# Moving raw-weight loads and cached-key loads in the wide-projection stage, and cutting the first weight part and the last output tile in halves

## Chip, cores and metric

The kernel runs on one core of a Trainium2 chip. The metric is the time of one execution in device microseconds; the median of several executions is compared. Besides that, one execution of the kernel is recorded by the hardware profiler, and all views of engines, waits and transfers come from that one.

The core has a matrix engine (TensorE, PE in the profile, with its weight loads as PEld), VectorE (DVE), ScalarE (ACT), GpSimd (POOL) and SyncE (SP). Each engine works through its own instructions in order. SyncE computes nothing here: it issues DMAs. A DMA can be issued from ScalarE's stream as well.

## The reference, cut to what matters

One step of a streaming encoder layer: 1024 frames of a new stream (the prompt) and 64 frames of a running stream (the sample), width 1024. All tokens go through one wide input projection of 6144 columns, two attention branches, and an output projection with a residual.

```python
h = rms_norm(x, norm_w) @ w_in                    # 1024 -> 6144 columns
sb_q, sb_k, sb_v, sb_z, cb_q, cb_k, cb_v, cb_z, g_sb, g_cb = jnp.split(h, SPLIT_POINTS, axis=-1)
...
o_sb = stick_breaking(q, k, v, q_pos, k_pos)      # branch A, 8 heads of 64
o_cb = band_attention(q, k, v, ..., rel_bias)     # branch B, 8 heads of 64
b_sb = (o_sb * jax.nn.silu(z_sb)) @ w_proj_sb
b_cb = (o_cb * jax.nn.silu(z_cb)) @ w_proj_cb
h = jax.nn.sigmoid(g_sb) * b_sb + jax.nn.sigmoid(g_cb) * b_cb
y = x + h @ w_out
```

For the sample, keys and values of 512 past frames (`cache_sb_k`, `cache_sb_v`, `cache_cb_k`, `cache_cb_v`) stand ahead of the new ones. Besides `y`, the keys and values of the new frames are outputs.

## The kernel before

The program is one straight list of instructions for each engine; loops are unrolled when it is built. Everything is computed to near float32 accuracy with a faster matmul type (`F32R`): each operand is split into a high part (`whi`, a copy rounded by ScalarE) and a low part (`wlo`, what is left, subtracted by VectorE or GpSimd), and three matmuls take the place of one.

**Stages.** From 0 to 42 us of the span the tokens are loaded in tiles of 128, normalized (`prep_s`: the square sum, `prep_a`: VectorE multiplies by the scale and the norm weight in two halves, giving `xn`) and transposed and split (`prep_b`); tile 8 is the sample's 64 rows, whose two parts go into `xs`, one half of the inner dimension after the other. The first matmul group needs `xs` and the first high part of the weights, made by `W.hi((0, 0))` at L117 as one activation of 128x1024. From there to 174 us go the six narrow blocks of projection columns in token-major order (`evac_nat` empties their accumulators at L503); from 174 to 217 the remaining value columns (L645). From 217 to 540 go the 14 *wide* column pairs, in channel-major order (L850). Then come attention, the branch projections, and from 890 the output projection (L1687).

**Wide pairs.** A pair is two blocks of 128 columns. It is computed from seven products `s` = 0 to 6 of half the size (a Strassen-like scheme with sums of weights and sums of tokens), 24 matmuls each. The first four pairs are keys and queries (`k`, `q`, `k`, `q`) of branch A, then come the `silu`, `sig` and `copy` pairs. For each product the loop builds, in this order: `prep(n + 5)` (high and low part of the weights five products ahead; ScalarE at L423, GpSimd), `presum(n + 6)` (sums `ws` of raw weights on VectorE, L391 and its neighbours), `step()`, one block of cached keys every third product, and then the matmuls and `emit`.

- `load_raw(n)` (L379) loads 512 KB of raw weights on SyncE into one of three buffers. It is called inside `presum` right behind the sum that reads the old contents, and inside `prep` right behind the high and low part that do.
- `soon(k, f)` puts off `f` to a later product's `step()`: `soon(0, f)` runs it in the next product, `soon(1, f)` in the one after. In this way stores stand in SyncE's stream behind the work that fills their buffers.
- `emit` writes results to an `hl` buffer (four of them) on ScalarE and VectorE (L750 for keys and queries) and stores it with `soon(0)` (by `rdma`, L51). For a key pair it also calls `out` with `soon(1)` or `soon(2)`: TensorE transposes, ScalarE copies to `ko` (L773), SyncE stores it (L775).
- `cache_load` (L708) loads a block `ck` of cached keys, 128 KB, on SyncE; `cache_part`, three products later, lets TensorE transpose it (L714), ScalarE and VectorE split it into `hc` (L716), a single buffer, and stores that with `soon(0)`. There are 16 such blocks, up to product 51.

`psF`, two accumulators named `acc`, serves both `out` and `cache_part`, so the transposes at L714 can wait for `ko` of two transposes before.

SyncE's stream is in order: a load that waits until its buffer has been read holds up all DMAs behind it. Each DMA's transfer itself goes on beside the others.

**Values of the sample.** For the sample's rows the high and low parts are stacked in 128 output rows; `fold` adds the two halves of 64 into `fl`, on ScalarE and VectorE. For value columns (`grp` 2 and 6) ScalarE copies `fl` to `vst`, from which two stores go.

**Last output tile.** The output projection has two column halves `i` of eight steps each; the last tile is `i` = 1, `s` = 6, `c` = 1: VectorE adds accumulator and `u2` over 128x512 (L1712) and `store_y` stores 256 KB on ScalarE's queue.

Of the kernel before, what the change touches and what calls it, by code (L numbers as in the profile page):

```python
# [8 lines left out]
F32 = mybir.dt.float32  # L9
F32R = mybir.dt.float32r  # L10
AF = mybir.ActivationFunctionType
# [21 lines left out]
def hybrid_step_kernel(ctx: ExitStack, tc: tile.TileContext, x_prompt, x_sample, c_sbk, c_sbv, c_cbk, c_cbv,  # L33
# [69 lines left out]
    class Weights:  # L103
# [7 lines left out]
            SP.dma_start(raw, src)  # L111
            self.raw[key] = (raw, pool, shape, extra)

        def hi(self, key):
            raw, pool, shape, extra = self.raw[key]
            h = pool.tile(shape, F32R, name="whi" + extra, bufs=2)
            A.activation(h, raw, AF.Copy)  # L117
            self.sp[key] = (h, None)

        def lo(self, key, eng=None):  # L120
# [80 lines left out]
    with ExitStack() as ph:  # L201
# [62 lines left out]
            A.activation(sq[:r], xts[t][:r], AF.Square, accum_out=ms[:r])  # L264
            rsqrt(rst[t][:r], ms[:r], 1.0 / D, 1)

        def prep_a(t):
            r = rows(t)
            xt = xts.pop(t)
            xn = p1.tile([128, D], F32, name="xn", bufs=2)  # L270
            for c in (slice(0, 512), slice(512, D)):
                V.scalar_tensor_tensor(xn[:r, c], xt[:r, c], rst[t][:r], nw[:r, c], op0=OP.mult, op1=OP.mult)
            xns[t] = xn

        xs = pn.tile([128, KT, 128], F32R, name="xs", bufs=1)

        def prep_b(t):
            r = rows(t)
            xn = xns.pop(t)
            for hf in range(2):  # L280
                pt = psT.tile([128, 4, 128], F32, name="pt")
                for k in range(4):
                    TE.transpose(pt[:, k, :r], xn[:r, (hf * 4 + k) * 128:(hf * 4 + k + 1) * 128], ident[:r, :r])  # L283
                if t == 8:
                    s = xs[:, hf * 4:hf * 4 + 4]
                    A.activation(s[:, :, 0:64], pt[:, :, :r], AF.Copy)
                    V.tensor_tensor(out=s[:, :, 64:128], in0=pt[:, :, :r], in1=s[:, :, 0:64].bitcast(F32),
                                    op=OP.subtract)
                    continue
                h, l = (xhl[s][hf][:, :, xc(t):xc(t) + r] for s in range(2))  # L290
                A.activation(h, pt[:, :, :r], AF.Copy)
                V.tensor_tensor(out=l, in0=pt[:, :, :r], in1=h.bitcast(F32), op=OP.subtract)
# [9 lines left out]
        def evac_nat(i, t, ps):  # L302
            r = rows(t)
            if t == 8:
                ps = fold(pn, ps)
            c0 = NB[i]
            grp = c0 // 512
            n0 = c0 % 512
            if grp in (2, 6):
                v = pn.tile([128, 256], F32, name="vst", bufs=3)  # L310
                A.activation(v[:r], ps[:r, :], AF.Copy)
                dst = d_sbv if grp == 2 else d_cbv
                SP.dma_start(dst[t * 128:t * 128 + r, n0:n0 + 256], v[:r])
# [55 lines left out]
        def load_raw(n):  # L369
# [8 lines left out]
                                                    bufs=1 if own else 2)  # L378
            SP.dma_start(raws[n], w_in[h * 512:(h + 1) * 512, c:c + 256].rearrange("(k p) n -> p k n", p=128))  # L379

        def presum(n):

            i, s = divmod(n, 7)
            if i >= len(pairs) or s not in (1, 4, 6):
                return
            a, b = slice(0, 128), slice(128, 256)
            r1, r2 = raws[2 * i], raws[2 * i + 1]

            def total(x, y, op):
                d = ws.tile([128, 4, 128], F32, name="ws")  # L390
                V.tensor_tensor(out=d, in0=x, in1=y, op=op)  # L391
                return d[:]

            if s == 1:
                sums[1] = total(r1[:, :, b], r2[:, :, b], OP.add)
                sums[2] = total(sums[1], r1[:, :, a], OP.subtract)
            elif s == 4:
                sums[3] = total(r1[:, :, a], r1[:, :, b], OP.subtract)
                load_raw(2 * i + 3)
            else:  # L400
                sums[4] = total(r2[:, :, a], sums[2], OP.subtract)

        def prep(n):
# [20 lines left out]
            (V if n == 1 else G).tensor_tensor(out=t[:, 1], in0=src, in1=t[:, 0].bitcast(F32), op=OP.subtract)  # L424
            blk[n] = t
            if s == 6:
                load_raw(2 * i + 4)

        load_x(3)
        idle = psA.tile([128, 512], F32, name="acc").rearrange("p (k n) -> p k n", n=128)  # L430
# [18 lines left out]
        prep_s(8)  # L449
        prep_a(8)  # L450
        prep_s(0)
        prep_b(8)
        beat(3)
        prep_a(0)
        W.hi((0, 0))
        W.hi((0, 1))
        W.lo((0, 0), V)
        W.lo((0, 1), V)
# [238 lines left out]
    with ExitStack() as ph:  # L697
# [7 lines left out]
        def cache_load(b, p, h):  # L705
            cks[b, p, h] = cq.tile([128, 2, 128], F32, name="ck")
            src = (c_sbk if b == "sb" else c_cbk)[256 * h:256 * h + 256, p * 128:(p + 1) * 128]
            SP.dma_start(cks[b, p, h], src.rearrange("(t p) c -> p t c", p=128))  # L708

        def cache_part(b, p, h):  # L710
            ck = cks.pop((b, p, h))
            pt = psF.tile([128, 512], F32, name="acc")[:, 0:256]
            for t in range(2):
                TE.transpose(pt[:, t * 128:(t + 1) * 128], ck[:, t], ident)  # L714
            hc = cq.tile([128, 2, 256], F32R, name="hc")
            A.activation(hc[:, 0], pt, AF.Copy)  # L716
            V.tensor_tensor(out=hc[:, 1], in0=pt, in1=hc[:, 0].bitcast(F32), op=OP.subtract)
            soon(0, lambda: rdma(d_cT[b][p][:, :, 256 * h:256 * h + 256], hc))

        later = []  # L720

        def soon(n, f):
            later.append([n, f])
# [90 lines left out]
        for n in range(1, LEAD):  # L814
            prep(n)
            presum(n + 1)
        presum(LEAD)
        right = [lambda s: xhl[s][0][:, :, 0:HF], lambda s: tms[1][s], lambda s: tms[0][s],
                 lambda s: xhl[s][1][:, :, 0:HF], lambda s: tms[2][s], lambda s: tms[3][s],
                 lambda s: xhl[s][1][:, :, HF:T]]  # L820
# [839 lines left out]
    for i in range(2):  # L1660
# [3 lines left out]
        for q, s in enumerate(OP_):  # L1664
# [14 lines left out]
            for c in range(2) if s != "b" else ():  # L1679
# [25 lines left out]
                if s in (3, 4, 5, 6):  # L1705
                    w, half = {3: (0, 0), 4: (1, 1), 5: (1, 0), 6: (0, 1)}[s]
                    ys.append(ys.pop(0))
                    y = ys[-1]
                    x = {3: xrs.pop((i, w, half, c)) if s == 3 else None, 4: None, 5: s1[c], 6: u2[c]}[s]
                    if s == 4:  # L1710
                        p, x = u3[c], xrs.pop((i, 1, 1, c))
                    V.tensor_tensor(out=y, in0=p, in1=x, op=OP.add)  # L1712
                    store_y(i, w, half, c, y)
            for s_, wh, wl in ([] if n == 0 else [(0,) + first, (3, wh, wl)] if n == 1 else
# [58 lines left out]
```

## Time and profile before

| what | us |
|---|---|
| median of 3 executions | 981.91 |
| lowest, highest of them | 981.41, 986.34 |
| the profiled execution's own time | 983.7 |
| its span, from the first to the last instruction | 981.8 |
| TensorE busy: 0 to 42 | 39.45 of 42 |
| 42 to 174 | 130.19 of 132 |
| 174 to 217 | 43.00 of 43 |
| 217 to 540 (the wide pairs) | 310.63 of 323 |
| 540 to 890 | 349.38 of 350 |
| 890 to 981.8 | 87.64 of 91.8 |

The 1.9 us between the profiled execution's time and its span lie ahead of the first and behind the last instruction. In the wide pairs GpSimd is busy for 156.85 us of 323, VectorE 142.40, ScalarE 120.47. The mean granted clock of TensorE over the span is 0.99 of full speed, and 0.97 in the wide pairs.

How to read the views: in a timeline a row is the start in us, the duration, the engine, the line of the kernel, the operation, `out<-in` by tile name with shapes, and in brackets how long the engine had stood idle and what released it. An engine with a `q` (SPq, ACTq) is that engine's DMA queue. In a list of waits a row is who waited, for whom, the total, the count and the longest. In a list of DMAs the last number is the median time from issue to landing.

### The profile page before, as it was taken

What the parts mean: (1) busy time and instruction counts of PE and PEld (TensorE: products, weight loads), DVE (VectorE), ACT (ScalarE), POOL (GpSimd) and SP (SyncE); (2) the same over time, 40 slices, a digit from 0 to 9 for tenths busy, and PEclk for the clock granted to TensorE, in tenths of its full rate; (3) what the DMA queues carried; (4) which work ended last, traced back from release to release, by engine and by line L of the source; (5) the groups of instructions that cost most, each with busy time, mean ns of one, the idle gap of its engine ahead of it and who ended that gap; (6) DMA issues with size and microseconds to landing.
All of it is one profiled execution on the core that took longest, in us unless ns stands there. A gap on an engine that the chain in (4) does not pass through costs nothing.

```text
span 981.8 us, 20460 instructions
## 1 busy us (share of the span) xinstructions
PE 960.3 (98%) x7591; PEld 912.5 (93%) x7591; DVE 605.0 (62%) x1209; ACT 476.5 (49%) x1054; POOL 366.1 (37%) x379
## 2 busy tenths in 40 slices
PE   8999999999998999999999999999999999999998
PEld 8999999998988899999999987878888888999998
DVE  6568888555453544544332187778677766489745
ACT  6534444414333433443333276667787775465320
POOL 3305455115342545665542310101341111586641
PEclk9999999998998999999999999999999999999999
DMA  6771454445565556655532897689699842862642
GB/s 220 230 262 47 148 167 135 141 135 182 150 200 168 179 188 192 212 179 177 158 98 87 232 265 217 164 225 245 194 277 277 248 135 62 257 185 96 208 139 82
DMA packets 180698, 175.77 MB, mean 179 GB/s; under 512 B 31018, under 2 KB 167086, under 8 KB 180599
## 3 DMA queue, kind: packets, MB, share of 16 engines
q1 hardware_dynamic: 169046, 159.45, 55.1%
q10 hardware_dynamic: 8736, 8.33, 2.7%
q0 software_dynamic: 2816, 6.69, 2.1%
q8 instruction: 60, 0.98, 0.4%
q14 instruction: 40, 0.32, 0.1%
HBM read 112.42 MB, written 62.00 MB: 178 GB/s over the span
## 4 chain that ended last, share of the span: by engine, by line
PE 84%; DVE 4%; DMA 4%; issue 3%; ACT 2%; SPq 2%; POOL 1%; ACTq 0%; DVEq 0%; POOLq 0%
PE b L850 23%; PE acc L503 10%; PE b L1687 8%; PE o L1367 7%; PE z L1275 7%; PE pt L1328 7%; PE acc L1126 5%; PE b L1168 5%; PE acc L1019 5%; PE v L645 3%; PE acc L645 1%; DMA ck<-in_cache_cb_k_dram 1%; DMA out_dram<-vst 1%; PE pt L283 1%; PE pk L355 1%
## 5 line engine op out<-in xcount | busy, mean ns | idle before, releaser
L1297 DVE TENSOR_TENSOR_SCAN be<-be,imp 128x128 f32<-128x128 f32 (+7 forms) x64 | 83.3, 1341 | 8.1 <-ACT be L1278 7.9
L1328 PE MATMUL pt<-ident,be 128*128 128x128 f32 (+1 forms) x568 | 87.7, 278 | 0.6 <-ACT wT L1337 0.4
L1275 PE MATMUL z<-ks,sq 128*128 128x320 f32 (+5 forms) x384 | 87.5, 338 | 0.0
L1328 PEld LDWEIGHTS pt<-ident,be 128*128 128x128 f32 (+1 forms) x568 | 65.7, 140 | 13.1 <-issue 4.6
L1337 ACT ACTIVATE wT<-pt 128x512 f32<-128x512 f32 (+3 forms) x123 | 56.9, 495 | 42.9 <-PE pt L1328 42.8
L858 DVE TENSOR_TENSOR u<-b,s 128x256 f32<-128x256 f32 (+1 forms) x56 | 24.2, 439 | 83.0 <-PE b L850 76.9
L1275 PEld LDWEIGHTS z<-ks,sq 128*128 128x128 f32 x384 | 63.6, 190 | 1.7
L1367 PE MATMUL o<-wT,vp 128*64 128x256 f32 (+1 forms) x608 | 64.2, 356 | 0.0
L1367 PEld LDWEIGHTS o<-wT,vp 128*64 128x64 f32 x608 | 40.3, 136 | 23.7 <-issue 7.5
L1300 ACT ACTIVATE be<-be,sm 128x640 f32<-128x640 f32 (+5 forms) x68 | 47.2, 694 | 17.2 <-DVE sm L1299 17.2
L424 POOL TENSOR_TENSOR whix<-ws,whix 128x512 fp32r<-128x512 f32 x28 | 37.0, 1320 | 47.8 <-ACT whix L423 43.9
L503 PE MATMUL acc<-whi,xa 128*128 128x256 f32 x192 | 52.6, 293 | 0.6 <-DVE fl L299 0.3
L503 PE MATMUL acc<-whi,xm 128*128 128x256 f32 x192 | 49.8, 279 | 0.0
L503 PE MATMUL acc<-wlo,xa 128*128 128x256 f32 x192 | 49.8, 279 | 0.0
L503 PE MATMUL acc<-whix,xm 128*128 128x256 f32 x192 | 49.8, 279 | 0.0
L503 PE MATMUL acc<-whix,xb 128*128 128x256 f32 x192 | 49.7, 278 | 0.0
L503 PE MATMUL acc<-wlox,xm 128*128 128x256 f32 x192 | 49.7, 279 | 0.0
L1288 ACT ACTIVATE be<-be,sm 128x640 f32<-128x640 f32 (+5 forms) x68 | 47.3, 695 | 5.0 <-DVE sm L1280 4.5
L1278 ACT ACTIVATE be<-z 128x384 f32<-128x384 f32 (+6 forms) x104 | 47.8, 512 | 3.2 <-PE z L1275 2.3
L923 POOL DMA_DIRECT2D d_osb<-zt x20 | 10.8, 542 | 101.2 <-DVE zt L1376 55.8
L850 PE MATMUL b<-xm,wlo 128*128 128x256 f32 (+1 forms) x224 | 46.9, 298 | 0.0
L424 POOL TENSOR_TENSOR wlo<-ws,wlo 128x512 fp32r<-128x512 f32 x27 | 37.0, 1371 | 26.3 <-ACT wlo L423 24.8
(397 smaller groups left out, 3286.4 us busy)
## 6 DMA issues: line engine op xcount, KB each, us to landing
wraw<-in_w_in_dram SPq DMA_DIRECT2D x31, 512.0 KB, 4.3
wrawx<-in_w_in_dram SPq DMA_DIRECT2D x16, 512.0 KB, 4.1
sq<-d_qsbT SPq DMA_DIRECT2D x32, 192.0 KB, 4.8
sq<-d_qcbT SPq DMA_DIRECT2D x32, 192.0 KB, 4.8
xt<-in_x_prompt_dram SPq DMA_DIRECT2D x8, 512.0 KB
d_kcbT<-hl SPq DMA_DIRECT2D x8, 512.0 KB
d_qcbT<-hl SPq DMA_DIRECT2D x8, 512.0 KB, 3.9
d_ksbT<-hl SPq DMA_DIRECT2D x16, 256.0 KB
```

What stands on the lines that cost most here:

```text
L424: (V if n == 1 else G).tensor_tensor(out=t[:, 1], in0=src, in1=t[:, 0].bitcast(F32), op=OP.subtract)
L503: TE.matmul(ps, x, w, start=first, stop=last)
L850: TE.matmul(ps[:, :m], w[:, hl_, k], right[s](x)[:, k, a:b], start=s < 3 and k == 0 and e == 0, stop=k == 3 and e == 2, skip_group_check=s ...
L1019: TE.matmul(ps[:, :b - a], w[:, k], xk(x, k)[:, a:b], start=k == 0 and n == 0, stop=k == KT - 1 and n == 2)
L1126: TE.matmul(ps[:, :e - a], w[:, p, cw], g[:, a:e], start=m % 12 == 0, stop=m % 12 == 11)
L1168: TE.matmul(pp[uu][:, :n], w[:, p, uu * 128:uu * 128 + 128], g[:, a:e], start=p == 0 and m == 0, stop=p == NPAIR - 1 and m == 2)
L1275: TE.matmul(z[:, :m], s[:, e, q0:q0 + 128], ks[:, h, o + x:o + y], start=(e, h) == parts[0], stop=(e, h) == parts[-1])
L1297: V.tensor_tensor_scan(be[:r, n - 1::-1], be[:r, n - 1::-1], im[:, ::-1], 0.0, op0=OP.mult, op1=OP.max)
L1328: TE.transpose(pt[:kr, x, :r], be[:r, kb * 128:kb * 128 + kr], ident[:r, :r])
L1337: A.activation(w[:, sl:sl + m, q0:q0 + r], pt[:, :m, :r], AF.Copy)
L1367: TE.matmul(o[hd * 64:hd * 64 + 64, c0:c1], vv[:kr, kb, hd * 64:hd * 64 + 64], wT[b, p, j, hd, s // 4][:kr, s % 4, c0:c1] if j < 4 else wT ...
L1687: TE.matmul(ps[:, t], left[s](xs_, k)[:, ts_], wt_[:, k], start=s < 3 and t == k == e == 0, stop=k == 3 and e == 2, skip_group_check=s > 2 ...
```

## The change

Six edits. Nothing that is computed changes, and TensorE's order of instructions is the same as before.

1. *Raw weights.* From the start of the wide loop on (`late_raw`), `load_raw` is called by `soon(1)` one product later than the sum or split that frees its buffer.
2. *Cached keys.* `cache_load` is issued from ScalarE's stream.
3. *The store of `hc`* goes by `soon(1)` in place of `soon(0)`.
4. *Start.* `W.hi((0, 0))` becomes two activations of 128x512; the first half of `xn` of tile 0 is computed between the two subtractions that make `xs`.
5. *Values of the sample* in the narrow blocks are stored straight from `fl`; two activations go.
6. *Last tile.* Two additions of 128x256, each followed by a store of 128 KB, one on ScalarE's queue and one on SyncE's.

```diff
-        def hi(self, key):
+        def hi(self, key, cuts=1):
             raw, pool, shape, extra = self.raw[key]
             h = pool.tile(shape, F32R, name="whi" + extra, bufs=2)
-            A.activation(h, raw, AF.Copy)
+            for j in range(cuts):
+                k = slice(shape[1] // cuts * j, shape[1] // cuts * (j + 1))
+                A.activation(h[:, k], raw[:, k], AF.Copy)
...
-        def prep_b(t):
+        def prep_b(t, between=None):
...
                     A.activation(s[:, :, 0:64], pt[:, :, :r], AF.Copy)
+                    if hf:
+                        between()
                     V.tensor_tensor(out=s[:, :, 64:128], in0=pt[:, :, :r], in1=s[:, :, 0:64].bitcast(F32),
...
-                v = pn.tile([128, 256], F32, name="vst", bufs=3)
-                A.activation(v[:r], ps[:r, :], AF.Copy)
+                v = ps if t == 8 else pn.tile([128, 256], F32, name="vst", bufs=3)
+                if t < 8:
+                    A.activation(v, ps, AF.Copy)
...
+        late_raw = [False]
+
+        def delayed(f):
+            if late_raw[0]:
+                soon(1, f)
+            else:
+                f()
...
-                load_raw(2 * i + 3)
+                delayed(lambda: load_raw(2 * i + 3))
...
-                load_raw(2 * i + 4)
+                delayed(lambda: load_raw(2 * i + 4))
...
-        prep_b(8)
+        prep_b(8, lambda: prep_a(0, (0,)))
         beat(3)
-        prep_a(0)
-        W.hi((0, 0))
+        prep_a(0, (1,))
+        W.hi((0, 0), 2)
...
-            SP.dma_start(cks[b, p, h], src.rearrange("(t p) c -> p t c", p=128))
+            A.dma_start(cks[b, p, h], src.rearrange("(t p) c -> p t c", p=128))
...
-            soon(0, lambda: rdma(d_cT[b][p][:, :, 256 * h:256 * h + 256], hc))
+            soon(1, lambda: rdma(d_cT[b][p][:, :, 256 * h:256 * h + 256], hc))
...
         presum(LEAD)
+        late_raw[0] = True
...
+                    if (i, s, c) == (1, 6, 1):
+                        a = 512 * half + 256 * c
+                        for t, eng in ((0, A), (1, SP)):
+                            V.tensor_tensor(out=y[:, t], in0=p[:, t], in1=x[:, t], op=OP.add)
+                            eng.dma_start(y_p[a + 128 * t:a + 128 * t + 128,
+                                              512 * i + 256 * w:512 * i + 256 * w + 256], y[:, t])
+                        continue
                     V.tensor_tensor(out=y, in0=p, in1=x, op=OP.add)
```

The order of the instructions at three places. In each row stand the line, the operation, `out<-in` by tile name with a buffer number, and the shape. First SyncE's stream in the third wide pair (the second of keys), near 289 us of the span before; `d_ksbT` is where keys of branch A are stored, `d_csbT` where cached keys are, `out_2` and `out_6` are the key outputs. Before:

```order
L51 DMA d_ksbT2_72<-hl_3981 256x1x32
L708 DMA ck_3998<-in_cache_sb_k_dram 128x2x128
L379 DMA wraw_4041<-in_w_in_dram 128x4x256
L775 DMA out_2_dram<-ko_4044 128x2x128
L772 DMA out_6_dram<-kos_4054 32x128
L775 DMA out_2_dram<-ko_4050 128x2x128
L51 DMA d_csbT2_80<-hc_3995 256x1x256
L51 DMA d_ksbT3_73<-hl_4029 256x1x256
L51 DMA d_ksbT3_73<-hl_4033 256x1x256
L51 DMA d_ksbT3_73<-hl_4033 256x1x32
```

And after the change, the same place:

```order
L51 DMA d_ksbT2_72<-hl_3978 256x1x32
L790 DMA out_2_dram<-ko_4039 128x2x128
L787 DMA out_6_dram<-kos_4049 32x128
L790 DMA out_2_dram<-ko_4045 128x2x128
L51 DMA d_ksbT3_73<-hl_4026 256x1x256
L51 DMA d_ksbT3_73<-hl_4030 256x1x256
L51 DMA d_ksbT3_73<-hl_4030 256x1x32
L51 DMA d_csbT2_80<-hc_3992 256x1x256
L790 DMA out_2_dram<-ko_4094 128x2x128
L787 DMA out_6_dram<-kos_4104 32x128
L790 DMA out_2_dram<-ko_4100 128x2x128
L386 DMA wraw_4109<-in_w_in_dram 128x4x256
```

The weight load has moved behind three key stores, three `hl` stores and the next product's key stores; the `hc` store behind the `hl` stores; the load of `ck` has left the stream.

Second, ScalarE's stream around the cached keys at the same place. Before:

```order
L423 ACTIVATE whix_3986<-ws_3918 128x512
L716 ACTIVATE hc_3995<-acc_3992 128x256
L750 ACTIVATE hl_4029<-u3_4012 128x256
L750 ACTIVATE hl_4033<-u3_4026 128x288
L423 ACTIVATE wlox_4036<-wraw_3750 128x512
L773 ACTIVATE ko_4044<-acc_4043 128x256
```

After:

```order
L438 ACTIVATE whix_3983<-ws_3913 128x512
L731 ACTIVATE hc_3992<-acc_3989 128x256
L723 DMA ck_3995<-in_cache_sb_k_dram 128x2x128
L765 ACTIVATE hl_4026<-u3_4009 128x256
L765 ACTIVATE hl_4030<-u3_4023 128x288
L438 ACTIVATE wlox_4033<-wraw_3793 128x512
L788 ACTIVATE ko_4039<-acc_4038 128x256
```

The key load now stands right behind the activation that follows the transposes of the block before; the rest keeps its order.

Third, VectorE at the start of the program, where `xs` is the sample's token tile and `wlo`, `wlox` the first low parts. Before:

```order
L272 SCALAR_TENSOR_TENSOR xn_230<-xt_177,rs_226,nw_208 64x512 x2
L287 TENSOR_TENSOR xs_194<-pt_239,xs_194 128x4x64
L287 TENSOR_TENSOR xs_194<-pt_246,xs_194 128x4x64
L272 SCALAR_TENSOR_TENSOR xn_256<-xt_181,rs_235,nw_208 128x512 x2
L124 TENSOR_TENSOR wlo_263<-wraw_183,whi_259 128x1024
L124 TENSOR_TENSOR wlox_265<-wrawx_185,whix_261 128x1024
```

After:

```order
L275 SCALAR_TENSOR_TENSOR xn_230<-xt_177,rs_226,nw_208 64x512 x2
L293 TENSOR_TENSOR xs_194<-pt_239,xs_194 128x4x64
L275 SCALAR_TENSOR_TENSOR xn_252<-xt_181,rs_235,nw_208 128x512
L293 TENSOR_TENSOR xs_194<-pt_246,xs_194 128x4x64
L275 SCALAR_TENSOR_TENSOR xn_252<-xt_181,rs_235,nw_208 128x512
L126 TENSOR_TENSOR wlo_264<-wraw_183,whi_259 128x1024
L126 TENSOR_TENSOR wlox_266<-wrawx_185,whix_262 128x1024
```

One half of `xn` of tile 0 has moved ahead of the second subtraction.

More of the change, by code (lines that the diff above doesn't have):

```diff
@@ L265, in prep_s, with prep_a @@
             rsqrt(rst[t][:r], ms[:r], 1.0 / D, 1)
-        def prep_a(t):
+        def prep_a(t, halves=(0, 1)):
             r = rows(t)
[L269 to L273, printed above, removed]
+            if t not in xns:
+                xns[t] = p1.tile([128, D], F32, name="xn", bufs=2)
+            for hf in halves:
+                c = slice(512 * hf, 512 * hf + 512)
+                V.scalar_tensor_tensor(xns[t][:r, c], xts[t][:r, c], rst[t][:r], nw[:r, c], op0=OP.mult, op1=OP.mult)
+            if halves[-1] == 1:
+                del xts[t]
         xs = pn.tile([128, KT, 128], F32R, name="xs", bufs=1)
-        def prep_b(t):
+        def prep_b(t, between=None):
             r = rows(t)
```

## The prediction, made before the changed kernel was run

> **What bounds the kernel now.** First the page's head, then the list of who waited for whom on TensorE, kept to the stage of the wide projections (217 to 540 us, 14 column pairs of seven products each), then busy time and granted clock by stretches.
>
> ```profile
> span 981.8 us, 20460 instructions
> PE 960.3 (98%) x7591; PEld 912.5 (93%) x7591; DVE 605.0 (62%) x1209; ACT 476.5 (49%) x1054; POOL 366.1 (37%) x379
> ```
>
> TensorE is busy 98% of the span, so only its gaps can be won, and what follows them. Nearly all of them stand at one line, the transposes of the cached keys (who waited for whom, total us, times, longest):
>
> ```profile
> PE acc L503 <- DVE wlox L124: 1.5, 1, 1.5
> PE acc L714 <- ACT ko L773: 7.4, 3, 4.8
> PE acc L714 <- DMA ck<-in_cache_cb_k_dram: 3.7, 3, 2.2
> PE acc L714 <- DMA ck<-in_cache_sb_k_dram: 1.0, 1, 1.0
> ```
>
> That is 12.1 us of idling at L714. It costs more than itself (stretch, its length, busy time and count on each engine, granted clock, DMA share, GB/s):
>
> ```profile
> 239.00:246.00 7.00, 6.26 (x29) 6.25 (x30) 1.75 (x5) 1.90 (x6) 1.28 (x1) 0.51 0.90 280
> 246.00:297.00 51.00, 46.11 (x369) 44.97 (x367) 23.34 (x51) 19.93 (x51) 19.88 (x14) 1.00 0.59 179
> 297.00:304.00 7.00, 5.89 (x27) 5.90 (x28) 1.48 (x3) 2.23 (x7) 1.63 (x1) 0.51 0.72 214
> 341.00:345.00 4.00, 4.00 (x22) 4.00 (x21) 2.24 (x5) 1.17 (x3) 1.63 (x1) 0.57 0.38 100
> 405.00:540.00 135.00, 135.00 (x1087) 135.00 (x1086) 50.55 (x98) 48.58 (x107) 69.34 (x61) 1.00 0.48 145
> ```
>
> At full clock a matmul of this stage takes 46.11/369 = 0.125 us; 135.00/1087 gives 0.124. After the three longest gaps the granted clock is about half. The 29, 27 and 22 matmuls there would have taken 3.6, 3.4 and 2.75 us, so the slow stretches cost 2.65, 2.5 and 1.25 us. The stage loses 12.1 + 6.4 = 18.5 us; from 405 to 540 it loses nothing.
>
> Why the keys and `ko` come late is read from the DMA queue's own waits on SyncE:
>
> ```profile
> SPq L379 <- DVE ws L391: 27.5, 8, 4.6
> ```
>
> Eight loads of raw weights stood 27.5 us at the queue's head, each until VectorE's sum had read the old contents of its buffer, and everything behind them stood too.
>
> **The change part by part.**
>
> *Cached keys on ScalarE's queue.* The third gap, 2.2 us before 340.5, shows the term: ScalarE finished the previous key block (`hc`) at 330.54, but SyncE came to the next key load at 334.01.
>
> ```profile
> 330.18 0.36 ACT L716 ACTIVATE hc<-acc 128x256 fp32r<-128x256 f32 x1
> 334.01 1.25 SPq L708 DMA_DIRECT2D ck<-in_cache_cb_k_dram  x1
> ck<-in_cache_sb_k_dram SPq DMA_DIRECT2D x8, 128.0 KB, 2.7
> ```
>
> In the changed order the load is the row right behind `hc`, so it starts at about 330.6 and lands by 333.3 at the median of 2.7 us. Had it taken twice that, it would land at 336, still ahead of the end of the product before the gap, 338.3. I take all four waits on the keys as gone: 3.7 + 1.0 = **4.7 us**, and the half-clock stretch of the third gap with it, **1.25 us**. The bounds are nothing and 5.95. The price is 16 triggers in ScalarE's stream, some 0.5 us each; ScalarE is busy 19.93 of 51 us there, so I count them at nothing. Without that cover each would push `hl` and `ko` back by half a microsecond, and the two gaps at `ko` with them: up to 1.0.
>
> *Raw weights a product later.* The longest gap, 4.8 us, ends with `ko`. SyncE's and ScalarE's rows before it:
>
> ```profile
> 289.15 0.37 SPq L379 DMA_DIRECT2D wraw<-in_w_in_dram  x1
> 289.61 0.46 SPq L775 DMA_DIRECT2D out_dram<-ko  x1
> 291.13 0.53 SPq L51 DMA_DIRECT2D d_csbT<-hc  x1
> 291.70 0.67 SPq L51 DMA_DIRECT2D d_ksbT<-hl  x1
> ...
> 288.41 0.37 ACT L773 ACTIVATE ko<-acc 128x256 f32<-128x256 f32 x1
> 295.50 0.42 ACT L750 ACTIVATE hl<-u 128x256 fp32r<-128x256 f32 x1 [2.89 <-DMA d_ksbT<-hl]
> 297.17 0.61 ACT L423 ACTIVATE whi<-wraw 128x512 fp32r<-128x512 f32 x1
> 297.69 0.36 ACT L773 ACTIVATE ko<-acc 128x256 f32<-128x256 f32 x1
> ...
> d_qsbT<-hl SPq DMA_DIRECT2D x16, 256.0 KB, 3.5
> ```
>
> The weight load issues at 289.15. Behind it come three `ko` stores, the `hc` store, and at 291.70 the store whose landing ScalarE needs at 295.50 to have an `hl` buffer again. Changed, the load and the `hc` store stand behind that store. The `ko` stores begin when the first `ko` is written, 288.8, and take 291.13 - 289.61 = 1.5 us; the store issues at about 290.3 and, by the median of the same shape, lands 3.5 us later, at 293.8. ScalarE goes on 1.7 us earlier, and so does all behind it: **1.7 us**, leaving 3.1 of the 4.8. That still exceeds the 2.2 us after which the clock halved, so I keep the slow stretch. Bounds: nothing, and 4.8 + 2.5 = 7.3.
>
> The trace halves the clock after idling of 2.2 us. The Trainium skill, "TensorE: Matmul & The Clock Gate", section "Why this matters for your kernels", asks only that gaps stay under about 3 us; the measured 0.51 after the first gap, 2.4 us long, speaks against it. By its figure that gap would have cost nothing beyond itself, and were the rest of the longest gap only 0.2 us shorter than I work out, the clock would stay whole and the time be 2.5 us lower.
>
> The first gap, before 239.74, I leave as it is. The chain of work that ended last shows what fills it:
>
> ```profile
> 237.93 0.45 DVE s L862
> 238.45 0.44 ACT hl L750
> 238.90 0.52 ACT whix L423
> 239.42 0.28 ACT ko L773
> ```
>
> VectorE and ScalarE hand each other one result after another, and the second `ko` comes last. No DMA stands in it and the order of these rows is unchanged, so its 2.4 + 2.65 us stay (bounds nothing and 5.1 gained, should idling fall otherwise over the clock's windows).
>
> What is late next? The delayed loads themselves. The tightest is this one:
>
> ```profile
> 412.17 0.40 SPq L379 DMA_DIRECT2D wraw<-in_w_in_dram  x1
> 420.87 3.50 DVE L391 TENSOR_TENSOR ws<-wraw 128x512 f32<-128x512 f32 x1
> wraw<-in_w_in_dram SPq DMA_DIRECT2D x31, 512.0 KB, 4.3
> ```
>
> A product later (24 matmuls, 3.0 us) it issues at 415.2 and lands at 419.5, 1.4 us before VectorE reads it. Behind a late sum stand VectorE's evacuations; the blocks are made five products (15 us) ahead. Nothing, then; at most some 2 us if several land late together.
>
> The `hc` store also moves back by a product, behind the product's three `hl` stores, and its single buffer gates the next `hc` on ScalarE:
>
> ```profile
> 374.31 0.42 ACT L744 ACTIVATE hl<-u 128x256 f32<-128x256 f32 x1 [4.03 <-DMA d_zcb<-hl]
> 383.40 0.38 ACT L716 ACTIVATE hc<-acc 128x256 fp32r<-128x256 f32 x1 [2.69 <-DMA d_ccbT<-hc]
> d_ccbT<-hc SPq DMA_DIRECT2D x8, 256.0 KB, 5.7
> ```
>
> Such a wait was there before: 2.7 us at 383.40, and one of 4.0 at 374.31, and neither shows among TensorE's waits, which at that place were for the key. Queued behind `hc` are the new key trigger, then `hl`, `ko` and the weights' high parts. I take nothing; the other end is the slower rival below.
>
> *Start.* TensorE waited 0.56 us for the first high part:
>
> ```profile
> 9.07 1.05 ACT L117 ACTIVATE whi<-wraw 128x1024 fp32r<-128x1024 f32 x1
> 10.18 0.75 PE L503 MATMUL acc<-whi,xs 128*128 128x256 f32 x4 [0.56 <-ACT whi L117]
> ```
>
> A half of 128x512 takes 0.61 (297.17 above), so the first half is ready 0.44 us earlier and the second about 0.1 later than the whole was; of four matmuls two can start early. I take **0.25 us** (bounds 0.1 lost, 0.56 gained). The sample's values straight from their sum remove two activations of 0.4 us in a stretch where TensorE's one wait, 1.5 us at L503, comes from a chain of VectorE work; nothing, at best 1.5.
>
> *Tail.* The last addition, its store, and the nearest rows for the halves:
>
> ```profile
> 977.67 0.69 DVE L1712 TENSOR_TENSOR xm<-b,xm 128x512 f32<-128x512 f32 x1 [2.03 <-PE b L1687]
> L858 DVE TENSOR_TENSOR u<-b,s 128x256 f32<-128x256 f32 (+1 forms) x56 | 24.2, 439 | 83.0 <-PE b L850 76.9
> out_dram<-xm ACTq DMA_DIRECT2D x16, 256.0 KB, 2.3
> out_dram<-ko SPq DMA_DIRECT2D x16, 128.0 KB, 1.8
> ```
>
> Two halves end 2 x 0.44 - 0.69 = 0.2 us after the whole; a store of half the size lands 0.5 us faster. **0.3 us** gained (bounds 0.2 lost, 0.5 gained). The Trainium skill, "DMA: Bandwidth & Descriptors", section "Rules for kernel authors", says two transfers to disjoint halves serialize on the same engines and advises against them; by it the tail gains nothing and the sum is 0.3 higher; no row here shows the pair.
>
> Sum: 4.7 + 1.25 + 1.7 + 0.25 + 0.3 = 8.2 us. The profiled execution took 983.7 us (span 981.8 and 1.9 around it), so 975.5 for one like it. It lies 1.8 above the median of 981.91, so the median becomes **973.7**.
>
> **The rivals.**
>
> *The rest of the longest gap falls under what halves the clock.* For it: gaps of 1.0 us and the 1.5 at L503 show no slow stretch, and if the store lands like `ko`'s, in 1.8, ScalarE goes on 3.4 us earlier, leaving 1.4. Against: the handoffs of the first gap alone fill 2.4. Price: another 1.7 + 2.5, so 969.5; with the first gap's slow stretch shifting away too, 967. Chance 0.20.
>
> *The change doesn't do what it says, since SyncE is short of issue time.* Three `hl` stores at 0.6 and three `ko` stores at 0.5 us fill a product of 3.0 us in the key pairs, loads or no loads. Then the longest gap stays (1.7 not won), and one more handoff like the first gap opens, 2.4 + 2.65: 973.7 + 6.75 = 980.4. Chance 0.17.
>
> *Slower: ScalarE is blocked as SyncE was.* The `hc` store issues some 5.5 us after `hc` (rest of the product, then three stores of 0.6) and the next `hc` is due 9 us after the last, so a landing of 5.7 already makes ScalarE wait 2.2 at each of the later blocks. It reaches TensorE when key load and landing (0.5 + 2.7) also end beyond the following transposes, that is from a landing of some 11 us, or from a wait beyond the 4.0 that was covered. Then each of seven later blocks costs about 1.1 us of gap and 1.25 of slow clock, and the 5 us won there are lost: 973.7 + 16.5 + 5 = 995. Chance 0.07.
>
> **How the numbers follow.** The forecast has 0.56, between 970 and 977; the rivals 0.20, 0.17 and 0.07. The range of 965 to 981.5 takes in the first two and leaves out the slower case and the full bounds. A measurement of this kernel tells some 0.5% from no change, 4.9 us: faster means below 977.0. Faster takes the first rival and nearly all of the forecast, 0.74; same is 0.18; slower 0.08.
>
> **What would show it.** No wait of L714 on `ck` in TensorE's list; one of about 2.4 us on `ko`, with its slow stretch, in the first key pair, and one of about 3 in the third; SyncE's wait for the sums shrunk from 27.5 us; the first product 0.25 us earlier; the last store landing within 2 us. It is wrong if ScalarE's waits on `hc` stores rise beyond 4 us, or if new gaps of TensorE appear after 405.

## The result, and the profile after

| | before | changed |
|---|---|---|
| median, us | 981.66 (980.89 to 986.34, 4 runs) | 970.5 (967.78 to 973.69, 4 runs) |
| ratio, 95% interval | | 0.9874 (0.984 to 0.9907) |
| profiled execution's own time, span | 983.7, 981.8 | 967.78, 966.0 |

The change gains 11.2 us at the median; 8.2 was forecast. The profiled execution of the changed kernel is the fastest of its four, so the pair of profiles shows more: 15.9 us. One execution of all those below, of the kernel with only the later `hc` store, ran at a granted clock of 0.56 and took 1563.87 us; it is left out.

TensorE's list of waits after the change (who waited for whom, us in total, times, longest):

```profile
PE acc L729 <- ACT ko L788: 4.7, 3, 2.4
PE acc L449 <- POOL half L239: 1.4, 1, 1.4
PE acc L518 <- DVE wlox L126: 1.1, 1, 1.1
PE pt L287 <- DVE xn L275: 0.6, 2, 0.4
PE b L866 <- DVE wlo L439: 0.2, 1, 0.2
PE pt L1344 <- ACT wT L1353: 0.2, 1, 0.2
PE pt L1344 <- DVE wT L1355: 0.2, 1, 0.2
```

L729 is the old L714. No wait for a cached key is left, and the longest wait for `ko` has fallen from 4.8 to 2.4 us. The two long waits that remain, in TensorE's timeline:

```profile
238.70 0.33 PE L729 MATMUL acc<-ident,ck 128*128 128x128 f32 x1 [2.44 <-ACT ko L788]
...
290.44 0.33 PE L729 MATMUL acc<-ident,ck 128*128 128x128 f32 x1 [2.11 <-ACT ko L788]
...
327.80 0.27 PE L729 MATMUL acc<-ident,ck 128*128 128x128 f32 x1
```

The same three transposes in the timeline before:

```profile
239.74 0.48 PE L714 MATMUL acc<-ident,ck 128*128 128x128 f32 x1 [2.43 <-ACT ko L773]
...
298.11 0.47 PE L714 MATMUL acc<-ident,ck 128*128 128x128 f32 x1 [4.82 <-ACT ko L773]
...
340.51 0.30 PE L714 MATMUL acc<-ident,ck 128*128 128x128 f32 x1 [2.23 <-DMA ck<-in_cache_cb_k_dram]
```

TensorE's order is the same in both kernels, so differences of such starts say where the time went: 1.04 us are won ahead of the first block, 7.67 by the second, 12.71 by the third. Of the 6.63 us between the first two, 2.71 are the shorter second gap and 1.0 the wait for a key of `sb` that is gone; of the 5.04 between the next two, 2.23 are the gap that is gone. Most of the rest is clock. Stretches of 7 us around both gaps after the change (length, busy time and count on each engine, granted clock, DMA share, GB/s):

```profile
236.30:243.30 7.00, 4.60 (x39) 4.59 (x40) 3.26 (x8) 3.17 (x10) 1.67 (x2) 1.00 0.82 209
288.30:295.30 7.00, 4.89 (x41) 4.86 (x41) 2.26 (x5) 3.73 (x10) 1.96 (x2) 1.00 0.92 268
389.00:524.00 135.00, 135.00 (x1082) 135.00 (x1081) 49.35 (x96) 48.91 (x107) 67.13 (x60) 1.00 0.47 143
```

The clock is 1.00 behind both, where it was 0.51 before. The last row is the gapless end of the wide pairs, 405 to 540 before: 1082 matmuls in 135 us where it was 1087, so about 0.6 us (5 of 0.124) is lost again without any wait; counted matmul by matmul in the last section it is 0.88.

SyncE's own wait, and ScalarE's waits for `hc` (same columns), after the change:

```profile
SPq L386 <- DVE ws L406: 4.3, 2, 3.0
...
ACT hc L731 <- DMA d_csbT<-hc: 6.8, 4, 3.0
...
ACT hc L731 <- DMA d_ccbT<-hc: 4.9, 3, 3.8
```

SyncE's wait for the weight sums fell from 27.5 to 4.3 us. ScalarE's wait for the stores of `hc` rose from 2.7 to 11.7 us; TensorE's list shows no wait that comes from it.

### The profile page after: what moved, and what is told of

The parts are those of the page before. It is cut to its first block, busy times and chain, and to the rows that moved or that the text cites. A ratio compares the mean times of both kernels' runs of the same rounds, so it can differ in the third digit from the quotient of the medians.

```text
span 966.0 us, 20468 instructions
## 1 busy us (share of the span) xinstructions
PE 953.2 (99%) x7591; PEld 906.3 (94%) x7591; DVE 605.8 (63%) x1210; ACT 476.6 (49%) x1053; POOL 364.4 (38%) x379
## 4 chain that ended last, share of the span: by engine, by line
PE 90%; DVE 4%; ACT 2%; DMA 1%; issue 1%; POOL 1%; SPq 1%; DVEq 0%; ACTq 0%; POOLq 0%
PE b L866 29%; PE acc L518 10%; PE b L1703 8%; PE o L1383 7%; PE z L1291 7%; PE pt L1344 7%; PE acc L1142 5%; PE b L1184 5%; PE acc L1035 5%; PE v L660 3%; PE acc L660 1%; PE pt L287 1%; DMA rb<-in_rel_bias_dram 1%; PE pk L362 1%; PE acc L1746 1%
## 5 line engine op out<-in xcount | busy, mean ns | idle before, releaser
L1184 PE MATMUL b<-og,whi 128*128 128x384 f32 (+1 forms) x192 | 46.7, 327 | 0.0
```

What stands on the lines that cost most here:

```text
L1184: TE.matmul(pp[uu][:, :n], w[:, p, uu * 128:uu * 128 + 128], g[:, a:e], start=p == 0 and m == 0, stop=p == NPAIR - 1 and m == 2)
```

## The experiments

Each kernel was timed beside the kernel before on one chip; there the kernel before had medians of 983.53 us (first four experiments), 982.56 (next four) and 982.85 (last two). Gaps are from the one profiled execution of each.

**Keys on ScalarE's queue alone.**

```diff
-            SP.dma_start(cks[b, p, h], src.rearrange("(t p) c -> p t c", p=128))
+            A.dma_start(cks[b, p, h], src.rearrange("(t p) c -> p t c", p=128))
```

> The kernel before with one edit: the loads of cached keys are issued by ScalarE. Theory (the raw-weight loads that wait at SyncE's head delay whatever stands behind them, key loads and hl stores alike): TensorE's waits for keys, 4.7 us in the profile before, are gone or under 0.5 us; the waits for ko stay at about 7.4 us with the longest at 4 to 5, since the hl stores still stand behind the weight loads. Time 3 to 6 us below before, 976 to 979. Rival (keys and ko are late for one common reason, TensorE meeting two accumulators with six transposes): the key waits turn into waits for ko at the same products, and the sum of idling at the key transposes stays near 12 us.

Measured 977.46 us, ratio 0.9941 (0.9919 to 0.9964), 5.8 us by the ratio. TensorE's waits at the key transposes:

```profile
PE acc L714 <- ACT ko L773: 7.4, 3, 4.8
```

It is the only row at L714: the key waits are gone and the `ko` waits untouched. The rival, by which one would turn into the other, falls.

**Late weight loads alone.**

```diff
-                load_raw(2 * i + 3)
+                delayed(lambda: load_raw(2 * i + 3))
...
-                load_raw(2 * i + 4)
+                delayed(lambda: load_raw(2 * i + 4))
...
         presum(LEAD)
+        late_raw[0] = True
```

> The kernel before with one edit: raw weights loaded a product later in the wide loop. Theory: SyncE's wait for VectorE's sums falls from 27.5 us to under 6, the longest gap shrinks from 4.8 us to 2 to 3, and because the key loads stood behind the same weight loads, the waits for keys shrink too, from 4.7 to under 2 us, without being moved to another queue. Time 5 to 9 us below before. Rival (key loads are late by their own place in SyncE's stream, behind key stores): waits for keys stay at 4 us or more, and only the longest gap shrinks; time 2 to 4 us below.

Measured 975.46, ratio 0.992 (0.9899 to 0.9942), 7.9 us.

```profile
PE acc L722 <- ACT ko L781: 5.5, 3, 2.9
PE acc L722 <- DMA ck<-in_cache_cb_k_dram: 2.9, 2, 1.5
```

SyncE's wait for the sums is 4.3 us, the longest gap 2.85. Key waits fell from 4.7 to 2.9: more than the rival had it, less than the theory. So part of the keys' lateness came from the weight loads ahead of them and part from their place in SyncE's stream; the gains of the two edits overlap.

**The later store of `hc` alone.**

```diff
-            soon(0, lambda: rdma(d_cT[b][p][:, :, 256 * h:256 * h + 256], hc))
+            soon(1, lambda: rdma(d_cT[b][p][:, :, 256 * h:256 * h + 256], hc))
```

> The kernel before with one edit: the store of the cached keys' parts goes a product later. Theory: it changes little by itself, the longest gap stays between 4 and 5 us, since the weight load still stands ahead of the hl stores; time within 2 us of before. Rival (it was this 256 KB store ahead of the hl stores that delayed their landing): the longest gap shrinks to 2 to 3 us with SyncE's wait for the sums still at 27 us.

Measured 983.63 (nine executions), ratio 1.0002 (0.9983 to 1.0022): nothing, as the theory had it. The rival falls: the longest gap stays near 4 us. The inside did change. ScalarE's waits for `hc` stores went from 2.7 us to 21.3:

```profile
ACT hc L716 <- DMA d_ccbT<-hc: 11.3, 3, 6.9
ACT hc L716 <- DMA d_csbT<-hc: 10.0, 3, 5.7
```

The longest `ko` gap fell by 0.8 to 3.98, and a new wait for VectorE's `u`, 1.7 us, came, with a key wait of 3.39; that gain and loss just cancel is read from this one profile.

**The edits at both ends alone** (edits 4 to 6 of the change).

```diff
-        prep_b(8)
+        prep_b(8, lambda: prep_a(0, (0,)))
...
-        W.hi((0, 0))
+        W.hi((0, 0), 2)
...
+                v = ps if t == 8 else pn.tile([128, 256], F32, name="vst", bufs=3)
...
+                        for t, eng in ((0, A), (1, SP)):
+                            V.tensor_tensor(out=y[:, t], in0=p[:, t], in1=x[:, t], op=OP.add)
```

> The kernel before with the three edits at the ends alone: first high part in halves with the token work between, the sample's values stored from their sum, last tile in halves. Theory: the first matmul group starts 0.3 to 0.7 us earlier, TensorE is 1.0 to 1.3 us ahead at 120 us of the span, the wide pairs keep 12 us of idling at the key transposes, and from TensorE's last matmul to the span's end it is 3.9 us in place of 4.1. Time 1 to 2 us below before, not to be told from the spread. Rival (it shifts the later gaps to another place, and that decides): the gaps at the key transposes change by over 2 us in sum.

Measured 980.23, ratio 0.9969 (0.9955 to 0.9984), 3.0 us, where 1 to 2 were expected. The profile accounts for a part: at the matmul that stood at 22.8 us before, TensorE is 0.8 us ahead; from its last matmul to the span's end it is 3.9 us in place of 4.1. It is only 0.4 ahead at 122 us, not 1.0. The gaps at the key transposes changed by about half a microsecond, so the rival falls. Some 1.4 us more lie, in this profile, between the first two key blocks: the slow stretch behind the first gap was 3.41 us long, where it was 6.83 before. How long that stretch is varies from profile to profile; what makes the rest of the 3.0 us in the median is not shown.

**Undoing one edit of the change at a time.** First the keys back on SyncE.

```diff
-            A.dma_start(cks[b, p, h], src.rearrange("(t p) c -> p t c", p=128))
+            SP.dma_start(cks[b, p, h], src.rearrange("(t p) c -> p t c", p=128))
```

> The changed kernel with one edit undone: cached keys loaded by SyncE again. Theory (late weight loads cleared only part of the key waits; the key load's own place behind the key stores makes the rest): TensorE waits for keys for 2 to 4 us again, the longest wait for ko stays near 2 to 3 us, time 1.5 to 4 us above the changed kernel. Rival (the late weight loads alone make keys timely when hc is stored later too): waits for keys under 1 us, time within 1 us of the changed kernel.

Measured 972.23, ratio 0.9898 (0.988 to 0.9915). One wait for a key of 1.3 us is back:

```profile
PE acc L729 <- DMA ck<-in_cache_cb_k_dram: 1.3, 1, 1.3
```

It lies between theory and rival. Alone the edit was worth 5.8 us; beside late weight loads it takes one wait of 1.3 us away, and in time 1.1 us by the ratio against the changed kernel in the last experiment (0.9887), which the intervals do not tell from nothing.

Then the weight loads back at their old place.

```diff
-        late_raw[0] = True
```

> The changed kernel with one edit undone: raw weights loaded at once again. Theory: no waits for keys (they are on ScalarE's queue), SyncE's wait for the sums back at 27 to 31 us, the longest wait for ko back at 4 to 5 us with a half-clock stretch behind it in every execution; time 3 to 6 us above the changed kernel. Rival (the later store of hc is what frees the hl stores): the longest wait for ko stays at 2 to 3 us and the time within 2 us of the changed kernel.

Measured 982.54, ratio 1.0003 (0.9985 to 1.0022): not part of the gain is lost but all of it, and the theory's "no waits for keys" is wrong. The longest `ko` wait is back at 4.0, so the rival falls too.

```profile
PE acc L729 <- ACT ko L788: 6.6, 3, 4.0
PE acc L729 <- DMA ck<-in_cache_cb_k_dram: 5.7, 3, 4.0
```

Key waits are longer than before the change, though the keys are on ScalarE's queue. The chain of one of them, from SyncE's, ScalarE's and TensorE's timelines:

```profile
309.52 1.18 SPq L51 DMA_DIRECT2D d_qsbT<-hl  x2
315.29 0.39 SPq L386 DMA_DIRECT2D wrawx<-in_w_in_dram  x1
...
317.65 7.61 SPq L51 DMA_DIRECT2D d_qsbT<-hl  x7
325.85 0.39 SPq L386 DMA_DIRECT2D wraw<-in_w_in_dram  x1
326.28 0.51 SPq L51 DMA_DIRECT2D d_csbT<-hc  x1
...
320.55 0.38 ACT L731 ACTIVATE hc<-acc 128x256 fp32r<-128x256 f32 x1 [2.47 <-DMA d_csbT<-hc]
...
331.91 0.38 ACT L731 ACTIVATE hc<-acc 128x256 fp32r<-128x256 f32 x1 [6.06 <-DMA d_csbT<-hc]
331.94 0.37 ACTq L723 DMA_DIRECT2D ck<-in_cache_cb_k_dram  x1
...
337.38 0.41 PE L729 MATMUL acc<-ident,ck 128*128 128x128 f32 x2 [4.04 <-DMA ck<-in_cache_cb_k_dram]
```

SyncE stands from 310.70 to 315.29 at a weight load, and all stores behind it are late. The store of `hc` (written from 320.55 on) stands right behind another weight load, issues at 326.28 and lands at 331.9. Until then ScalarE stands 6.06 us at the next `hc`, with the key load queued behind it; the key lands 5.4 us after its issue, and TensorE has waited 4.04. In the changed kernel the same store has the weight load behind it, and ScalarE goes on 3.5 us after its issue:

```profile
317.78 0.63 SPq L51 DMA_DIRECT2D d_csbT<-hc  x1
...
321.30 0.38 ACT L731 ACTIVATE hc<-acc 128x256 fp32r<-128x256 f32 x1 [2.98 <-DMA d_csbT<-hc]
```

The later store of `hc` has carried the blockage from SyncE to ScalarE: with the keys moved alone, the `hc` store early and the weight loads not late either, no key was waited for (first experiment). So beside the later `hc` store, the key's new queue stays free only with late weight loads.

Last the store of `hc` a product earlier again.

```diff
-            soon(1, lambda: rdma(d_cT[b][p][:, :, 256 * h:256 * h + 256], hc))
+            soon(0, lambda: rdma(d_cT[b][p][:, :, 256 * h:256 * h + 256], hc))
```

> The changed kernel with one edit undone: the parts of the cached keys are stored a product earlier again, ahead of the hl stores. Theory: a second-order effect; the longest wait for ko goes from 2.1 to at most 2.9 us, as with the late weight loads alone; ScalarE's waits for its single hc buffer shrink; time within 2 us of the changed kernel. Rival (with the weight loads gone this store is the one thing ahead of the hl stores, and it decides): the longest wait is 3.5 us or more, time 3 us or more above.

Measured 973.43 (970.46 to 973.83), ratio 0.9898 (0.9876 to 0.992), by the ratio 1.1 us above the changed kernel in the last experiment, within the noise. The second gap is 2.85 us, as with the late loads alone, and ScalarE waits for no `hc` store:

```profile
292.86 0.44 PE L729 MATMUL acc<-ident,ck 128*128 128x128 f32 x2 [2.85 <-ACT ko L788]
```

A second-order effect, as expected: the later store is worth 0.7 us at one gap.

**Cached-key blocks where no keys of branch A are transposed.** The remaining gaps stand where two transposes of `out` for each half and those of `cache_part` share the two accumulators of `psF`.

```diff
+        CAT = [8, 11, 14, 17] + list(range(22, 56, 3))
...
-                if n >= 6 and n % 3 == 0 and (n - 6) // 3 < len(cjobs):
-                    cache_part(*cjobs[(n - 6) // 3])
-                    if (n - 3) // 3 < len(cjobs):
-                        cache_load(*cjobs[(n - 3) // 3])
+                if n in CAT:
+                    j = CAT.index(n)
+                    cache_part(*cjobs[j])
+                    if j + 1 < len(cjobs):
+                        cache_load(*cjobs[j + 1])
```

> The changed kernel, and the 16 blocks of cached keys placed at products 8, 11, 14, 17 and then 22, 25 to 55, in which no keys of branch A are transposed, in place of every third from 6 on. Theory (the two gaps that are left come from six transposes that share two accumulators within one product, and the spread of the changed kernel, 967.8 to 973.7, comes from whether these gaps halve the clock): both waits for ko, 2.4 and 2.1 us, are gone, no half-clock stretch is left but the one at the end, the time is 962 to 965 and its spread is under 3 us. Rival (VectorE and ScalarE are short of time in the key pairs, whatever is asked there): waits of 2 us or more appear at the moved transposes or at the accumulators that follow, and the time is 967 or more.

Measured 967.98 (967.08 to 970.49), ratio 0.9857 (0.9837 to 0.9876). Both `ko` waits are gone and the profile has no slow stretch before the end, but a new wait has come and the time is over 967, as the rival said; the theory's 962 to 965 is missed:

```profile
PE b L868 <- DVE u L876: 3.9, 4, 1.9
...
ACT hc L732 <- DMA d_ccbT<-hc: 6.0, 3, 3.8
...
ACT hc L732 <- DMA d_csbT<-hc: 3.6, 2, 2.1
```

In the timeline of its longest piece, ScalarE stands 4.20 us at `hc`, VectorE behind it at the `hc` subtraction, and the evacuation `u` behind that. The profile puts this one wait down to a matmul; at five other blocks it is the last `hc`'s store, 9.6 us in sum. Whether the store is the cause, and not the rival's lack of time on VectorE, the next experiment tries.

**The same with the store of `hc` as before the change**, and the changed kernel once more beside it.

```diff
         CAT = [8, 11, 14, 17] + list(range(22, 56, 3))
...
-            soon(1, lambda: rdma(d_cT[b][p][:, :, 256 * h:256 * h + 256], hc))
+            soon(0, lambda: rdma(d_cT[b][p][:, :, 256 * h:256 * h + 256], hc))
```

> The changed kernel with the cached-key blocks at products 8, 11, 14, 17, 22, 25 to 55, and the hc store a product earlier again, as before the change. Theory (the 3.9 us that TensorE waited for VectorE's u with the moved blocks come from ScalarE, and VectorE behind it, standing at the next hc until the late store of the last one has landed): ScalarE's waits for hc stores, 9.6 us there, fall under 3, TensorE's waits for u under 1 us, no slow clock before the end, time 963 to 965.5, some 4 us below the kernel with the moved blocks alone. Rival (the u waits come from VectorE's own load, two weight sums of 2.2 us and the hc subtraction in one product): they stay at 3 us or more, and the time stays at 967 to 968.

Measured **965.29** (963.17 to 967.49), ratio 0.9827 (0.9806 to 0.9848), the best of all: 6.5 us below the changed kernel beside it.

```profile
PE b L868 <- DVE u L876: 1.6, 2, 1.0
...
ACT hc L732 <- DMA d_csbT<-hc: 3.6, 2, 2.0
```

Both waits fall by more than half, if less than the theory asked (under 1 and under 3), and the time is 2.9 us by the ratios below the moved blocks alone, where some 4 were expected. The rival (waits of 3 us or more, 967 to 968) falls. The granted clock is 1.00 in all five executions.

> The changed kernel again, beside the improved one on one chip. Theory (its two gaps of 2.4 and 2.1 us always come, but halve the clock only where they fill some half of one of the clock's 3.41 us windows): both gaps are there again within 0.1 us, 0 to 2 slow stretches follow them, executions lie between 967.5 and 974 and the slower ones show the lower mean clock; median 970 to 972. Rival (the spread comes from transfers, with gaps of other lengths each time): the gaps differ by over 0.5 us from those of the first profile.

Measured 971.78 (969.35 to 972.06), ratio 0.9887 (0.9869 to 0.9906). The gaps are 2.44 and 2.15 us, so their lengths repeat within 0.05 and the rival falls. That the slower executions show the lower clock did not come: all four have 0.998, so the clock makes little of the 2.7 us between them. This time one slow stretch of 3.41 us follows the first (7 us around each gap; the clock is the third number from the end of the row):

```profile
236.60:243.60 7.00, 4.56 (x25) 4.52 (x25) 2.65 (x6) 2.61 (x8) 1.74 (x2) 0.76 0.80 223
289.90:296.90 7.00, 4.85 (x41) 4.57 (x39) 2.28 (x5) 3.70 (x11) 1.99 (x2) 1.00 0.92 261
```

## Why the prediction was right, and where its sizes were off

The direction, the range (965 to 981.5) and the mechanism held: SyncE's queue, blocked at its head by weight loads, made keys and `ko` late. By its steps:

- *Keys, 4.7 + 1.25 us.* Held: all four waits and the slow stretch are gone. What this part did not see is a condition. It asked whether sixteen triggers would push ScalarE's work; that a trigger stands behind an `hc` which waits for its own store is only in the part on the `hc` store and in the slower rival, and neither says that the late loads keep this wait short. With the later `hc` store and without the late loads the key waits come back at 5.7 us.
- *Late weight loads, 1.7 us, leaving 3.1.* Mis-sized. The gap fell to 2.11 (2.15 when repeated). The forecast let the `hl` store land 3.5 us after its issue, the median of its shape. The changed kernel's ScalarE and SyncE rows show 2.6:

```profile
285.24 1.87 SPq L51 DMA_DIRECT2D d_ksbT<-hl  x3
...
287.83 0.42 ACT L765 ACTIVATE hl<-u 128x256 fp32r<-128x256 f32 x1 [0.24 <-DMA d_ksbT<-hl]
```

  With 0.9 less the forecast would have left 2.2. In two parts: 4.8 to 2.85 by the loads (alone, and with `hc` undone), 2.85 to 2.1 by the later `hc` store.
- *The slow stretch behind that gap, kept at 2.5 us.* This step failed. "That still exceeds the 2.2 us after which the clock halved" took the length of a gap for what decides. In neither profile of the changed kernel did the clock halve behind it. Where the gap falls in the clock's windows decides (last section). By the counts there, a gap of 2.11 us puts 1.95 us (57% of a window, from where on all halved the clock) into one window in about half of its positions. So one slow stretch in two executions is the estimate, and that none came in either profile is in part luck. In time this is the first rival's outcome (969.5, chance 0.20), though the gap stayed longer than its 1.4 us; the measured 970.5 lies nearer to it than to the forecast's 973.7.
- *The first gap, 2.4 + 2.65 us, left as it is.* The gap held to 0.01 us; its slow stretch came in one of two profiles, and was half as long as before. The prediction had this only as a bound.
- *The `hc` store, nothing.* ScalarE's waits rose to 11.7 us, the longest 3.8, under the 4.0 that the prediction had seen covered; TensorE's list shows none of it. The sign of being wrong, waits beyond 4 us, thus came in the sum and not in a single wait, and did no harm. The slower rival's mechanism is real: it stands in the kernel without late loads, where it ate the whole gain, but at that price and not at the 21.5 us given. Its condition was off as well: by its own terms (5.5 us to the issue, 0.5 and 2.7 for the key, against 18) a landing beyond 9.3 us is needed, not of 11, and measured were 5.6, behind an `hc` that was already 2.47 late.
- *Delayed loads, nothing.* Held. VectorE's sums waited once for a weight load, 1.4 us (1.5 before), and TensorE not at all from 389 us to the end of the stage (the row of 135.00 us above):

```profile
DVE ws L406 <- DMA wraw<-in_w_in_dram: 1.4, 1, 1.4
```

- *Start, 0.25 us.* Too small. The first group starts at 9.49 in place of 10.18:

```profile
8.82 1.14 ACT L119 ACTIVATE whi<-wraw 128x512 fp32r<-128x512 f32 x2
9.49 0.30 PEld L518 LDWEIGHTS acc<-whi,xs 128*128 128x128 f32 x2 [0.32 <-ACT whi L119]
9.49 1.03 PE L518 MATMUL acc<-whi,xs 128*128 128x256 f32 x4
```

  TensorE's matmuls no longer wait there (the weight load, PEld, still does, 0.32), a wait of 0.25 us at 21.15 is gone too, and at the matmul that stood at 22.8 us before, the eight profiles with the edit are 0.4 to 1.0 us ahead, the three others from 0.2 ahead to 0.15 behind. The sample's values showed nothing, as forecast.
- *Tail, 0.3 us.* From TensorE's last matmul to the span's end it took 3.9 us in all eight profiles with the halves and 4.1 to 4.6 in the four without: 0.2 or more. The rule that the prediction cited from the Trainium skill, "DMA: Bandwidth & Descriptors", "Rules for kernel authors", expects no gain of two transfers (8.2 less 0.3, a gain of 7.9 us); it speaks of halves of the partitions, while each half here has all 128, so this case does not decide it.

Forecast 8.2; 11.2 measured, 11.1 when repeated. The third-pair gap gives 1.0 more and the start some 0.5. The other 1.5 us go with slow stretches that came less often than the forecast had them (it kept 2.65 and 2.5 us of them), part of which TensorE's rhythm (last section) takes back; this last split is argued from two profiles and not tried by itself.

## What to carry to other kernels

Put a DMA that must wait for a buffer behind those that others wait for, and look at what stands ahead of a DMA in its new queue before it is moved: the same edit was worth 5.8 us alone and some 1 us, within the noise, beside the late loads, and in the kernel with the later `hc` store and without late loads the key waits were longer than before the change. Edits to queues do not add: alone they gave 5.8, 7.9, 0 and 3.0 us, 16.7 in sum, together 11. And a collision on a buffer is better scheduled away than served faster: moving the key blocks to other products, with the `hc` store left early, won another 6.5 us.

## What the runs showed of the hardware

**The clock goes by windows, not by gaps.** In every trace the changes of the granted clock lie on a grid of 3.413 us, with another offset from the span's start each time (6.93 us before, 5.48 after, 7.91 when repeated). Each stretch of TensorE's idling was laid over the grid of its own trace, in twelve profiles, the first window and the program's end (behind 960 us) left out. Each step of the grid is a window, and its share of idling is compared with the clock of the next. Of 48 windows at full clock with more than 0.9 us of idling, none of the 29 with 49% or less was followed by a slow one; of the four at 51 to 55%, two were and two were not; of the 15 from 57% up, all were. One gap of 2.44 us thus did nothing where the grid cut it into 1.32 and 1.12 us, and halved the clock where it lay in one window, 72% of it. In a window that was slow already less was enough: idling of 21% to 42% was followed by another slow one (five cases), 3% or less never. The Trainium skill, "TensorE: Matmul & The Clock Gate", section "What's actually happening", has the free-running window of about 3413 ns, and the trace agrees; its advice to keep gaps under about 3 us ("Why this matters for your kernels") does not hold here: gaps of 1.95 to 2.44 us halved the clock in ten cases.

**TensorE has rhythms.** The 1015 matmuls from 412 to 538 us of the span before have no wait in any of the twelve profiles. They took 126.04 us in five of them and 126.92 in seven, and nothing between; between 440 and 480 us, matmuls that start 117 or 118 ns after the one before are 75 of 322 in the faster rhythm (before) and 110 of 320 in the slower (after). The output stage, 702 matmuls, took 79.56 to 81.70 us, its short waits (up to 0.7 us) included, and not just two values. The five executions of the best kernel, all at full clock, still spread over 4.3 us; that such rhythms are the reason is likely, but not shown. What sets the rhythm stays open; no run here tried it.
